# First MLP product by seven products of quarters instead of eight, in three of four chunks of inner features

## The chip, the cores and the metric

The kernel runs on one core of one Trainium2 chip. The metric is the device time of one execution, in microseconds (us): 1731.39 us before the change, the median of three runs (1730.09 to 1732.92). A core has five instruction queues that run at the same time and wait for each other by semaphores: PE (matrix products, with its weight loads, PEld), DVE (vector), ACT (scalar), POOL, and SP, which here issues DMAs. Each queue works through its list in order.

## The reference

The program is a decoder trunk of two layers over 512 tokens and 16 meta tokens, with 1024 features. Layer 0 mixes tokens by retention and gated DeltaNet heads, layer 1 by a Mamba-2 mixer. Behind each mixer comes a squared-ReLU MLP with 4096 inner features, and every sublayer ends in x <- LayerNorm(alpha * x + f(x)). The part that matters here:

```
def sq_relu_mlp(h, w1, w2):
    return jnp.square(jax.nn.relu(h @ w1)) @ w2

for i in range(DEPTH):                      # DEPTH = 2
    mix = retention_gdn_mixer(h, ...) if i % 2 == 0 else mamba2_mixer(h, ...)
    h = layer_norm(DN_ALPHA * h + mix, ln1_w[i], ln1_b[i])
    h = layer_norm(DN_ALPHA * h + sq_relu_mlp(h, mlp_w1[i], mlp_w2[i]), ln2_w[i], ln2_b[i])
```

All data are float32.

## The kernel before

Activations lie with features on the 128 partitions and tokens along the free dimension: 528 columns in layer 0 (two halves of 272 and 256) and 512 in layer 1 (behind its mixer the meta tokens are dropped). Each float32 operand is split in two tiles, a rounded high part and the low rest. A product of two operands then takes three matrix products (`mm3`, L172 to L175): high by high, high by low, low by high. Here "product" always means one of these PE instructions, and "split" the pair of a cast on ACT (L152) and a subtraction on DVE (L153).

A weight tile is 128 rows by 1024 columns, loaded by SP into one of two `wr` buffers (`fetch`), and split in two pieces of 512 columns into six `wh` and six `wl` buffers. A tile gives 128 output features and holds eight blocks of 128 inner features, so one output tile takes 8 x 3 = 24 products per stream of tokens: in layer 0 two streams (272 and 256 columns), in layer 1 one of 512 columns.

`mlp` (L376) goes over four chunks `c` of 1024 inner features. In each chunk `phase` makes eight tiles of the first product from `h` (names `hh`, `hl`), and `evac_u` turns each sum in PSUM into `u`: relu on ACT (L381), square in full precision on POOL (L383), the square's high part on ACT (L389), its low part on DVE (L390). Then a second `phase` makes eight tiles of the second product from `u`, and `evac0` (from `residual`, L363, or L367 and L368 in chunk 0) adds them on DVE to the residual sums, of which 16 tiles of the tag `m` stay in use through the whole MLP. The tags and their numbers of buffers: `s` 40 (528 columns), `m` 20, `row` 3, PSUM `mm` (names pmm) 3 and `mx` (names pmx) 5.

The order of instructions is made when the program is built: a scheduler gives each engine its list, in order of program and of readiness by its own estimate, so instructions of later tiles can stand ahead of earlier ones. On the chip that list is kept. `spawn` adds a generator whose stages are emitted one at each `tick`, between two parts of a product.

Up to the second products of layer 0's first MLP chunk the changed program has the same lists on every engine, apart from line numbers, and SP's list of DMAs is the same throughout.

Of the kernel before, what the change touches and what calls it, by code (L numbers as in the profile page):

```python
# [12 lines left out]
F32 = mybir.dt.float32  # L13
# [5 lines left out]
P = 128  # L19
# [19 lines left out]
PP_LN = 0  # L39
# [18 lines left out]
def trunk(ctx: ExitStack, tc: tile.TileContext, a, out):  # L58
# [68 lines left out]
    # ---------------------------------------------------------------- constants  # L127
# [22 lines left out]
    # ---------------------------------------------------------------- weights  # L150
# [26 lines left out]
    def product(o, blks, xs, m=P, k0=0, k1=None, every=8):  # L177
        """o[m, n] += sum over k0 <= k < k1 of blks[k]^T xs[k]"""
# [9 lines left out]
    def phase(tiles, rhs, evac, ns, head=0, tail=0, ready=None):  # L188
        """tiles: list of (srcs, key[, m]); rhs[half][k] = (hi, lo) APs, rhs[2] both halves where they fit a
        bank. In the first and the last tiles the halves are apart, so that what precedes and follows can  # L190
        work on one half at a time."""
# [28 lines left out]
    def jobs(lst, rhs, ns, **kw):  # L220
        """phase whose tiles bring their own evac"""
        phase(lst, rhs, lambda ev, hf, o: ev(hf, o), ns, **kw)

    # ---------------------------------------------------------------- h: hi/lo in two halves
# [3 lines left out]
    def parts(pair, spans):  # L228
        """(hi, lo) over the spans of both tiles"""
        return [tuple(x[:, o:o + n] for x in pair) for o, n in spans]  # L230

    # while the first loads are under way, products of zeros let the clock of the tensor engine come up
# [26 lines left out]
    def layernorm(r, ns, hf, go, apply, together=False):  # L259
        """statistics of the tokens of a half as its sums r come, then apply(off, bn, pt, mean, rstd, i)"""  # L260
# [49 lines left out]
    def norm_after(r, ns, wcol, bcol):  # L310
        """tasks for both halves, each from when its sums have been emitted"""
# [35 lines left out]
    def residual(hx, offs, ns, early=()):  # L347
        """evac into r = alpha * h + product"""
# [24 lines left out]
    def mlp(l, hx, ns, ready, r, evac0):  # L373
        w1, w2 = a["mw1"], a["mw2"]
        for c in range(4):
            u = [[None] * 8 for _ in hx]  # L376

            def evac_u(f, hf, o):
                n = ns[hf]
# [4 lines left out]
                if hf == 0:  # L384
                    pair = tl("s", L, F32R), tl("s", L, F32R)
                    for dst, x in zip(u, parts(pair, ((0, n), (n, ns[1]), (0, 512)))):
                        dst[f] = x
                hi, lo = u[hf][f]
# [3 lines left out]
            phase([([w1[l, c * 8 + f]], f) for f in range(8)], hx, evac_u, ns,  # L392
                  head=3 if c == 0 else 0, ready=ready if c == 0 else None)
            phase([([w2[l, c, m]], m) for m in range(KT)], u,
                  lambda m, hf, o: evac0(m, hf, o, last=c == 3), ns, tail=3 if c == 3 else 0)

    # ---------------------------------------------------------------- shared pieces
# [15 lines left out]
    def conv_job(src, wc, bcol, done):  # L413
        """projection through conv and silu, feature-major [128, L]"""
# [30 lines left out]
    def gate_job(src, width, task):  # L445
        """small projection, then a task on its sums"""
# [10 lines left out]
    def gate_task(fm, width):  # L457
        """token-major [128, 5, width] with unused rows zero"""
# [9 lines left out]
    def decay(dt_in, bias, alog, nh):  # L468
        """g = -exp(A_log) softplus(x + bias), sums over chunks and their exponentials"""
# [17 lines left out]
    # ================================================================ layer 0 mixer  # L487
# [475 lines left out]
    def hb(ap):  # L963
        """[128, heads] over the 64 features of a head"""
        return bc(ap, 64)
# [353 lines left out]
```

## Time and profile before

| | |
|---|---|
| median of three runs | 1731.39 us |
| the profiled execution, from its first to its last instruction | 1727.4 us |
| difference, around the span | 4.0 us |
| granted PE clock over the span | 0.995 of full speed |
| DVE splits of 512 columns (L153), whole program | 498, 759 ns on average |
| POOL squares (L383) | 128, 729 ns on average |
| relu out of PSUM (L381) | 128, 380 ns on average |
| bytes moved by DMA | 157.99 MB |

Layer 0's MLP runs from about 515 to 890 us of the span, layer 1's from about 1365 us to its end. A profile row of a timeline gives the start and the duration in us, the engine, the source line, the operation, and the tiles written <- read; "x2" means that two instructions were merged in the row, and a bracket tells how long the engine was idle ahead of it and what ended that. A row of the table by stretches gives, for each of PE, PEld, DVE, ACT and POOL in that order, the busy time and the number of instructions in the stretch, then the granted PE clock, the mean busy share of the DMA engines and GB/s. Busy times of PE overlap, since its products are pipelined; what counts for PE is the distance from start to start.

### The profile page before, as it was taken

The numbers are of one execution on the slowest core, as the hardware profiler recorded it, in microseconds if no ns is written. First come the engines' busy times: TensorE is split into PE (matmuls) and PEld (weight loads), VectorE is DVE, ScalarE is ACT, GpSimd is POOL, SyncE is SP. The second block draws the span as 40 slices with busy tenths as digits, with TensorE's granted clock in tenths as the row PEclk, the third lists the DMA queues.
The fourth block names the chain that finished last, engine by engine and source line by source line (L and its number), as shares of the span: only waits on it lengthen the run. The fifth ranks groups of instructions, "written<-read, shape, count | busy, mean of one in ns | idle before, by whom it ended". The sixth has DMA issues, their size and how long they took to land.

```text
span 1727.4 us, 29456 instructions
## 1 busy us (share of the span) xinstructions
PE 1690.1 (98%) x11644; PEld 1537.0 (89%) x11644; DVE 1015.5 (59%) x2116; ACT 680.0 (39%) x1455; POOL 324.1 (19%) x380
## 2 busy tenths in 40 slices
PE   9999999999999999999999999999999999999997
PEld 8899998899999999999999878888788888888886
DVE  6896667676436443343348767868753744444345
ACT  4432345554225333242425634554432533333331
POOL 1311211010004111010202245242400411101012
PEclk9999999999999999999999999999999999999999
DMA  7224211112222222222221443333222222222221
GB/s 252 69 86 121 77 63 62 38 63 85 98 66 82 92 92 87 98 87 89 96 72 61 131 133 88 99 110 111 80 79 98 73 86 98 98 98 89 94 98 61
DMA packets 80325, 157.99 MB, mean 91 GB/s; under 512 B 12668, under 2 KB 45820, under 8 KB 79932
## 3 DMA queue, kind: packets, MB, share of 16 engines
q1 hardware_dynamic: 80044, 155.86, 28.2%
q8 instruction: 91, 1.49, 0.4%
q14 instruction: 46, 0.38, 0.1%
q10 hardware_dynamic: 144, 0.26, 0.0%
HBM read 149.95 MB, written 6.15 MB: 90 GB/s over the span
## 4 chain that ended last, share of the span: by engine, by line
PE 84%; DVE 6%; DMA 3%; POOL 3%; ACT 2%; issue 2%; SPq 0%; POOLq 0%; DVEq 0%; ACTq 0%
PE pmm L173 24%; PE pmm L175 24%; PE pmm L174 24%; DMA row<-rd 2%; DVE s L407 2%; DVE wl L153 2%; POOL row L985 1%; PE pmx L271 1%; POOL hl L341 1%; DMA wr<-in_w 1%; PE pmx L331 1%; PE pmx L1049 1%; PE pmx L1045 1%; POOL n L147 1%; PE pmx L753 1%
## 5 line engine op out<-in xcount | busy, mean ns | idle before, releaser
L173 PE MATMUL pmm<-hh,wh 128*128 128x272 f32 (+4 forms) x2104 | 652.3, 311 | 2.3 <-ACT wh L152 0.9
L174 PE MATMUL pmm<-hl,wh 128*128 128x272 f32 (+4 forms) x2104 | 638.5, 304 | 2.7 <-POOL hl L341 2.1
L175 PE MATMUL pmm<-hh,wl 128*128 128x272 f32 (+4 forms) x2104 | 640.3, 304 | 0.1
L153 DVE TENSOR_TENSOR wl<-wr,wh 128x512 fp32r<-128x512 f32 (+1 forms) x498 | 376.2, 759 | 319.8 <-ACT wh L152 313.5
L152 ACT CAST wh<-wr 128x512 fp32r<-128x512 f32 (+1 forms) x498 | 306.6, 619 | 628.3 <-PE pmm L174 605.1
L173 PEld LDWEIGHTS pmm<-hh,wh 128*128 128x128 f32 (+2 forms) x2104 | 393.5, 187 | 25.0 <-issue 4.4
L174 PEld LDWEIGHTS pmm<-hl,wh 128*128 128x128 f32 (+2 forms) x2104 | 393.6, 187 | 24.4 <-POOL hl L341 4.6
L175 PEld LDWEIGHTS pmm<-hh,wl 128*128 128x128 f32 (+2 forms) x2104 | 393.5, 187 | 17.0 <-DVE wl L153 0.3
L173 PE MATMUL pmm<-s,wh 128*128 128x256 f32 (+2 forms) x1192 | 377.9, 317 | 0.0
L175 PE MATMUL pmm<-s,wl 128*128 128x256 f32 (+2 forms) x1192 | 377.2, 317 | 0.0
L174 PE MATMUL pmm<-s,wh 128*128 128x256 f32 (+2 forms) x1192 | 376.4, 316 | 0.0
L174 PEld LDWEIGHTS pmm<-s,wh 128*128 128x128 f32 x1192 | 224.3, 188 | 15.5 <-DVE s L1124 0.3
L173 PEld LDWEIGHTS pmm<-s,wh 128*128 128x128 f32 x1192 | 224.4, 188 | 15.1
L175 PEld LDWEIGHTS pmm<-s,wl 128*128 128x128 f32 x1192 | 224.1, 188 | 15.0
L383 POOL TENSOR_TENSOR m<-m 128x256 f32<-128x256 f32 (+1 forms) x128 | 92.1, 729 | 536.0 <-ACT m L381 532.7
L147 POOL TENSOR_TENSOR n<-n,neg 128x1 f32<-128x1 f32 (+2 forms) x58 | 37.9, 657 | 462.7 <-DVE n L146 436.5
L390 DVE TENSOR_TENSOR s<-m,s 128x256 fp32r<-128x256 f32 (+1 forms) x128 | 64.3, 521 | 95.2 <-POOL m L383 93.2
L407 DVE SCALAR_TENSOR_TENSOR s<-s,pp,s 128x528 f32<-128x528 f32 x120 | 96.5, 804 | 25.8 <-ACT s L405 24.1
L363 DVE TENSOR_TENSOR m<-m,pmm 128x256 f32<-128x256 f32 (+1 forms) x108 | 43.7, 423 | 107.4 <-PE pmm L175 107.2
L381 ACT ACTIVATE m<-pmm 128x256 f32<-128x256 f32 (+1 forms) x128 | 48.7, 380 | 60.4 <-PE pmm L175 60.4
L985 POOL TENSOR_TENSOR row<-row,m 128x1024 f32<-128x1024 f32 x16 | 32.8, 2052 | 122.3 <-DMA row<-rd 78.3
L389 ACT ACTIVATE s<-m 128x256 fp32r<-128x256 f32 (+1 forms) x128 | 54.0, 422 | 3.9
(275 smaller groups left out, 1501.1 us busy)
## 6 DMA issues: line engine op xcount, KB each, us to landing
wr<-in_mw SPq DMA_DIRECT2D x128, 512.0 KB, 3.3
wr<-in_w SPq DMA_DIRECT2D x88, 512.0 KB, 3.3
wr<-in_wo SPq DMA_DIRECT2D x29, 512.0 KB, 3.5
row<-rd SPq DMA_DIRECT2D x16, 512.0 KB, 6.0
s<-rd SPq DMA_DIRECT2D x32, 128.0 KB, 6.1
out<-row SPq DMA_DIRECT2D x7, 256.0 KB, 2.0
wr<-in_wo SPq DMA_DIRECT2D x6, 256.0 KB, 3.0
dt<-row SPq DMA_DIRECT2D x3, 365.5 KB, 5.9
```

What stands on the lines that cost most here:

```text
L147: G.tensor_tensor(dst, t, neg5[0:part, 0:n], op=POW)
L152: S.copy(dst_hi, src)
L153: V.tensor_tensor(dst_lo, src, dst_hi.bitcast(F32), op=SUB)
L173: T.matmul(o, w[0], x[0], start=first, stop=False)
L174: T.matmul(o, w[0], x[1], start=False, stop=False)
L175: T.matmul(o, w[1], x[0], start=False, stop=last)
L381: S.activation(t, o, AF.Relu)
L383: G.tensor_tensor(q, t, t, op=MUL)
L389: S.activation(hi, t, AF.Square)
L390: V.tensor_tensor(lo, q, hi.bitcast(F32), op=SUB)
L407: V.scalar_tensor_tensor(acc, cin[:, k:k + L], w[k], acc, op0=MUL, op1=ADD)
L985: G.tensor_tensor(g3(rw, 8), g3(rw, 8), bc(gc[:, c * 32 + 8 * g:c * 32 + 8 * g + 8], P), op=SUB)
```

## The change

For chunks 1 to 3 of each MLP (24 output tiles of the first product in a layer), two weight tiles and the whole token stream are taken together as a product of 2 x 2 blocks. The weight blocks are a11, a12 (tile f, inner blocks 0 to 3 and 4 to 7) and a21, a22 (tile f + 4); the blocks of h are its eight feature blocks in two groups of four, cut in two equal halves of tokens (`nh` = 264 columns in layer 0, 256 in layer 1). The blocks are combined as in Winograd's form of Strassen's method, in seven block products instead of eight:

- four sums of weight blocks for each pair of tiles: S1 = a21 + a22 and S3 = a11 - a21 on DVE, S2 = S1 - a11 and S4 = a12 - S2 on POOL, each 512 columns;
- four combinations of the blocks of h, made once in each layer (`combos`): for each of four feature blocks four steps, each a subtraction on POOL, one or two sums on DVE, and a split;
- seven block products of 4 x 3 = 12 products, 84 for a pair of tiles, where there were 96 (layer 0) or 48 of twice the width (layer 1);
- the results put together by a copy on ACT (L439) and five sums out of PSUM on DVE (L441, L445, L447, L454, L458), then `evac_u` as before on four pieces.

The order of the seven on PE in the source is a11 (first part of one output), S2, S3, S1, a12, a22, S4. The splits of S1 to S4 go to tiles of the tag `s`, eight for a pair; 16 more such tiles hold the combinations of h until the MLP ends. `p1` and `u3` are `m` tiles that hold partial sums.

```diff
+    def sevens(srcs, keys, B, nh, evac):
+        raw1, raw2 = fetch(srcs[0]), fetch(srcs[1])
+        a11, a12, a21, a22 = [x[:, i:i + 512] for x in (raw1, raw2) for i in (0, 512)]
+        s12, s34 = tl("row", 1024), tl("row", 1024)
+        s1, s2, s3, s4 = [x[:, i:i + 512] for x in (s12, s34) for i in (0, 512)]
+        V.tensor_tensor(s1, a21, a22, op=ADD)
+        V.tensor_tensor(s3, a11, a21, op=SUB)
+        G.tensor_tensor(s2, s1, a11, op=SUB)
+        G.tensor_tensor(s4, a12, s2, op=SUB)
...
+        bank = [pm(nh)] + [px(nh) for _ in range(3)]
...
+        w11 = pair(a11, False)
+        prod(bank[0], w11, 0, True, False)
+        p1 = tl("m", nh)
+        S.copy(p1, bank[0])
+        prod(bank[1], pair(s2, True), 5, True, True)
+        V.tensor_tensor(p1, p1, bank[1], op=ADD)
+        tick()
+        prod(bank[2], pair(s3, True), 6, True, False)
+        u3 = tl("m", nh)
+        V.tensor_tensor(u3, p1, bank[2], op=ADD)
+        prod(bank[3], pair(s1, True), 4, True, False)
+        V.tensor_tensor(u3, u3, bank[3], op=ADD)
+        evac(keys[1], 1, u3)
+        tick()
+        prod(bank[0], pair(a12, False), 1, False, True)
+        evac(keys[0], 0, bank[0])
+        prod(bank[2], pair(a22, False), 3, False, True)
+        c21 = tl("m", nh)
+        V.tensor_tensor(c21, p1, bank[2], op=ADD)
+        evac(keys[1], 0, c21)
+        tick()
+        prod(bank[3], pair(s4, True), 2, False, True)
+        V.tensor_tensor(p1, p1, bank[3], op=ADD)
+        evac(keys[0], 1, p1)
+        tick()
...
-            phase([([w1[l, c * 8 + f]], f) for f in range(8)], hx, evac_u, ns,
-                  head=3 if c == 0 else 0, ready=ready if c == 0 else None)
+            if c == 0:
+                phase([([w1[l, f]], f) for f in range(8)], hx, evac_u, ns, head=3, ready=ready)
...
+                spawn(combos(pairs, nh, get))
+                B += [[half(k, 0) for k in range(4)], [half(k, 0) for k in range(4, 8)],
+                      [half(k, 1) for k in range(4, 8)], tt[3], tt[0], tt[1], tt[2]]
+            else:
+                for f in range(4):
+                    sevens([w1[l, c * 8 + f], w1[l, c * 8 + f + 4]], (f, f + 4), B, nh,
+                           lambda f, hf, o: evac_u(f, hf, o, nh))
```

and the combinations of h, one of four such rounds:

```diff
+    def combos(pairs, nh, get):
...
+        for k in range(4):
+            d1, d3, e = tl("m", nh), tl("m", nh), tl("m", nh)
+            G.tensor_tensor(d1, part(k, 1, 0), part(k, 0, 0), op=SUB)
+            V.tensor_tensor(e, part(k, 1, 1), part(k, 0, 1), op=SUB)
+            V.tensor_tensor(d1, d1, e, op=ADD)
+            get(0, k, d1)
+            yield
...
+            d2, d4 = tl("m", nh), tl("m", nh)
+            G.tensor_tensor(d2, part(k + 4, 1, 0), d1, op=SUB)
+            V.tensor_tensor(d2, d2, part(k + 4, 1, 1), op=ADD)
+            get(1, k, d2)
+            yield
```

How the lists change is shown at three places. The number behind a name is that of the buffer.

First, DVE in the first product of layer 0's chunk 2, before: two tiles, of which each brings two splits of weights (L153) and two low parts of u (L390).

```order
L153 TENSOR_TENSOR wl1629_8194<-wr1627_8191,wh1628_8193 128x512
L153 TENSOR_TENSOR wl1631_8198<-wr1627_8191,wh1630_8197 128x512
L390 TENSOR_TENSOR s1597_8009<-m1600_8039,s1596_8008 128x256
L390 TENSOR_TENSOR s1610_8083<-m1608_8080,s1609_8082 128x272
L153 TENSOR_TENSOR wl1642_8268<-wr1640_8265,wh1641_8267 128x512
L153 TENSOR_TENSOR wl1644_8272<-wr1640_8265,wh1643_8271 128x512
L390 TENSOR_TENSOR s1610_8083<-m1613_8113,s1609_8082 128x256
L390 TENSOR_TENSOR s1623_8157<-m1621_8154,s1622_8156 128x272
```

The same place of the changed kernel, from the third to the fourth pair of the chunk. Ahead of these rows stand the split of S2 of the third pair, L458 of the second, the split of S3 of the third and L413 for the fourth.

```order
L153 TENSOR_TENSOR s1919_9619<-row1904_9555,s1918_9618 128x512
L486 TENSOR_TENSOR s1892_9501<-m1901_9547,s1891_9500 128x264
L441 TENSOR_TENSOR m1912_9581<-m1912_9581,pmx1907_9562 128x264
L414 TENSOR_TENSOR row1942_9719<-wr1939_9714,wr1940_9716 128x512
L445 TENSOR_TENSOR m1917_9616<-m1912_9581,pmx1908_9563 128x264
L447 TENSOR_TENSOR m1917_9616<-m1917_9616,pmx1909_9564 128x264
L486 TENSOR_TENSOR s1923_9640<-m1921_9637,s1922_9639 128x264
L486 TENSOR_TENSOR s1929_9664<-m1927_9661,s1928_9663 128x264
L153 TENSOR_TENSOR s1936_9692<-row1905_9556,s1935_9691 128x512
L454 TENSOR_TENSOR m1932_9683<-m1912_9581,pmx1908_9563 128x264
L153 TENSOR_TENSOR wl1978_9880<-wr1976_9877,wh1977_9879 128x512
L153 TENSOR_TENSOR s1951_9747<-row1941_9718,s1950_9746 128x512
```

Where before only splits and low parts alternated, the splits of S1 (first row), S4 (s1936) and the next pair's S2 (last row) now stand behind sums that read PSUM (pmx) and behind low parts of u (now L486) that need POOL's square.

Second, PE in the same chunk, from the first pair to the second, after the change. The banks are pmm1869 and pmx1870 of the second pair and pmm1906 of the third.

```order
L433 MATMUL pmm1869_9398<-hh1358_6667,wl1874_9403 128x264
L433 MATMUL pmx1870_9399<-s1539_7564,s1876_9420 128x264 [waits Activation_49]
L433 MATMUL pmx1870_9399<-s1539_7564,s1876_9420 128x264
L433 MATMUL pmm1906_9561<-hh1346_6637,wh1910_9565 128x264
L433 MATMUL pmm1906_9561<-hl1347_6638,wh1910_9565 128x264
L433 MATMUL pmm1906_9561<-hh1346_6637,wl1911_9566 128x264
L433 MATMUL pmm1906_9561<-hh1350_6647,wh1910_9565 128x264
L433 MATMUL pmm1906_9561<-hl1351_6648,wh1910_9565 128x264
L433 MATMUL pmx1870_9399<-s1539_7564,s1877_9421 128x264 [waits DVE_49]
```

Five products of the third pair's a11 stand between the first two of S2 (pmx1870, high part s1876) and its third, which waits for the low part s1877 from DVE; before, each tile's 24 products stood together, and this place has no counterpart there.

Third, DVE beside the second products of layer 0's chunk 0, one tile, before:

```order
L367 SCALAR_TENSOR_TENSOR m1567_7806<-hh1366_6687,pmm1566_7781 128x272
L368 SCALAR_TENSOR_TENSOR m1567_7806<-hl1367_6688,m1567_7806 128x272
L153 TENSOR_TENSOR wl1590_7972<-wr1588_7969,wh1589_7971 128x512
L367 SCALAR_TENSOR_TENSOR m1569_7834<-hh1366_6687,pmm1568_7809 128x256
L368 SCALAR_TENSOR_TENSOR m1569_7834<-hl1367_6688,m1569_7834 128x256
L153 TENSOR_TENSOR wl1592_7976<-wr1588_7969,wh1591_7975 128x512
```

and after:

```order
L367 SCALAR_TENSOR_TENSOR m1563_7716<-hh1358_6667,pmm1562_7691 128x272
L398 TENSOR_TENSOR m1564_7719<-m1564_7719,hl1367_6688 128x264
L368 SCALAR_TENSOR_TENSOR m1563_7716<-hl1359_6668,m1563_7716 128x272
L153 TENSOR_TENSOR s1566_7723<-m1564_7719,s1566_7723 128x264
L153 TENSOR_TENSOR wl1599_7921<-wr1597_7918,wh1598_7920 128x512
L367 SCALAR_TENSOR_TENSOR m1568_7751<-hh1358_6667,pmm1567_7726 128x256
L402 TENSOR_TENSOR m1565_7720<-m1565_7720,hl1367_6688 128x264
L368 SCALAR_TENSOR_TENSOR m1568_7751<-hl1359_6668,m1568_7751 128x256
L153 TENSOR_TENSOR wl1601_7925<-wr1597_7918,wh1600_7924 128x512
L153 TENSOR_TENSOR s1569_7756<-m1565_7720,s1569_7756 128x264
```

Each tile has got two steps of the combinations: a sum (L398, L402) behind POOL's subtraction, and the low part of a split of 264 columns.

More of the change, by code (lines that the diff above doesn't have):

```diff
@@ L371, in residual, with part, diff @@
         return r, evac
-    def mlp(l, hx, ns, ready, r, evac0):
+    def combos(pairs, nh, get):
+        q = slice(0, nh), slice(nh, 2 * nh)
+        def part(k, c, lo):
+            return pairs[k][lo][:, q[c]].bitcast(F32)
+        def diff(out, a, b, engine):
+            engine.tensor_tensor(out, a, b, op=SUB)
+        for k in range(4):
[5 more added lines that the diff above has]
+            yield
+            G.tensor_tensor(d3, part(k + 4, 1, 0), part(k, 1, 0), op=SUB)
+            V.tensor_tensor(e, part(k + 4, 1, 1), part(k, 1, 1), op=SUB)
+            V.tensor_tensor(d3, d3, e, op=ADD)
+            get(2, k, d3)
+            yield
[3 more added lines that the diff above has]
+            get(1, k, d2)
+            yield
+            G.tensor_tensor(d4, part(k + 4, 0, 0), d2, op=SUB)
+            V.tensor_tensor(d4, d4, part(k + 4, 0, 1), op=ADD)
+            get(3, k, d4)
+            yield
@@ new lines, in sevens, with pair, prod @@
+    def sevens(srcs, keys, B, nh, evac):
[7 more added lines that the diff above has]
+        G.tensor_tensor(s4, a12, s2, op=SUB)
+        def pair(x, big):
+            if big:
+                hi, lo = tl("s", 512, F32R), tl("s", 512, F32R)
+            else:
+                hi = sb.tile([P, 512], F32R, tag="wh", bufs=6, name=nm("wh"))
+                lo = sb.tile([P, 512], F32R, tag="wl", bufs=6, name=nm("wl"))
+            split(hi, lo, x)
+            return hi, lo
+        bank = [pm(nh)] + [px(nh) for _ in range(3)]
+        def prod(o, w, b, first, last):
+            for k in range(4):
+                c = slice(k * P, (k + 1) * P)
+                for i, (x, y) in enumerate(((0, 0), (0, 1), (1, 0))):
+                    T.matmul(o, w[x][:, c], B[b][k][y], start=first and k == i == 0, stop=last and k == 3 and i == 2,
+                             skip_group_check=True)
+        w11 = pair(a11, False)
[23 more added lines that the diff above has]
+        tick()
@@ L374, in mlp, with evac_u @@
+    def mlp(l, hx, ns, ready, r, evac0, pairs):
         w1, w2 = a["mw1"], a["mw2"]
+        nh = (ns[0] + ns[1]) // 2
+        B = []
         for c in range(4):
             u = [[None] * 8 for _ in hx]
-            def evac_u(f, hf, o):
-                n = ns[hf]
+            us = [None] * 8
+            def evac_u(f, hf, o, n=None):
+                off = 0
+                if n is None:
+                    n, off = ns[hf], hf * ns[0]
+                else:
+                    off = hf * n
@@ L926, in trunk @@
     r, ev = residual(h, (0, 0), ns0, early=range(5, KT))
-    hn, _, ready = norm_after(r, ns0, PP_LN, PP_LN + 8)
+    hn, hp, ready = norm_after(r, ns0, PP_LN, PP_LN + 8)
     phase([([a["wo0"][m, :, 0:1024], a["wo0"][m, :, 1024:2048]], m) for m in range(KT)], y, ev, ns0, tail=2)
@@ L931, in trunk @@
     hn, hx, ready1 = norm_after(r, ns0, PP_LN + 16, PP_LN + 24)
-    mlp(0, h, ns0, ready, r, ev)
+    mlp(0, h, ns0, ready, r, ev, hp)
     h = hn
@@ L1152, in trunk @@
     r, ev = residual(h, (16, 0), ns1, early=range(5, KT))
-    hn, _, ready = norm_after(r, ns1, PP_LN + 32, PP_LN + 40)
+    hn, hp, ready = norm_after(r, ns1, PP_LN + 32, PP_LN + 40)
     until(lambda: yw[2][11] is not None)
@@ L1216, in trunk @@
     spawn(finish(1))
-    mlp(1, h, ns1, ready, r, ev)
+    mlp(1, h, ns1, ready, r, ev, hp)
     drain()
```

18 lines of the change are left out of this document (14 added, 4 removed).

## The prediction

> **What bounds the kernel now.** I read the engine totals first, then the chain that ended last, then the stages the change touches.
>
> ```profile
> span 1727.4 us, 29456 instructions
> PE 1690.1 (98%) x11644; PEld 1537.0 (89%) x11644; DVE 1015.5 (59%) x2116; ACT 680.0 (39%) x1455; POOL 324.1 (19%) x380
> PE 84%; DVE 6%; DMA 3%; POOL 3%; ACT 2%; issue 2%; SPq 0%; POOLq 0%; DVEq 0%; ACTq 0%
> ```
>
> TensorE (PE) holds 84% of the chain. The share says nothing of the first MLP products, so next comes the table by stretches: a stretch of layer 0's first products (feature chunk 1), two tiles of layer 1's, and DVE's rows in each.
>
> ```profile
> core 0: us, PE busy (x) PEld busy (x) DVE busy (x) ACT busy (x) POOL busy (x), PEclk, DMA share, GB/s
> 623.60:670.50 46.90, 46.90 (x385) 46.90 (x385) 18.32 (x33) 21.45 (x46) 10.98 (x15) 1.00 0.28 91
> 1456.50:1467.60 11.10, 11.10 (x49) 9.02 (x49) 5.09 (x9) 5.27 (x13) 2.82 (x4) 1.00 0.28 95
> ...
> 628.69 0.44 DVE L390 TENSOR_TENSOR s<-m,s 128x272 fp32r<-128x272 f32 x1 [2.75 <-POOL m L383]
> 634.56 0.44 DVE L390 TENSOR_TENSOR s<-m,s 128x272 fp32r<-128x272 f32 x1 [2.07 <-POOL m L383]
> ...
> 1462.02 0.69 DVE L153 TENSOR_TENSOR wl<-wr,wh 128x512 fp32r<-128x512 f32 x1 [2.08 <-ACT wh L152]
> 1467.57 0.69 DVE L153 TENSOR_TENSOR wl<-wr,wh 128x512 fp32r<-128x512 f32 x1 [2.08 <-ACT wh L152]
> ```
>
> PE never stops there, and DVE is busy 18.32 of 46.90 us. The same DVE instruction recurs every 5.87 us in layer 0 (634.56 - 628.69) and every 5.55 us in layer 1: one feature tile. So a pair of tiles costs 11.74 and 11.10 us, all of it PE. A shorter product helps only while the other engines keep up.
>
> **What is removed.** A pair has 96 products of 256 or 272 columns in layer 0 (11.74 / 96 = 0.122 us each) and 48 of 512 in layer 1 (11.10 / 48 = 0.231 us). The change issues 84 per pair, of 264 columns (0.122) and of 256. The price of 256 is read in layer 1's last tiles:
>
> ```profile
> 1699.19 0.28 PE L174 MATMUL pmm<-s,wh 128*128 128x256 f32 x1
> 1704.50 0.28 PE L174 MATMUL pmm<-s,wh 128*128 128x256 f32 x1
> ```
>
> These are 45 products apart: 5.31 / 45 = 0.118 us. PE work per pair falls to 84 x 0.122 = 10.27 us (-1.47) and 84 x 0.118 = 9.91 us (-1.19). Twelve pairs a layer: 17.6 + 14.3 = **31.9 us less PE work**.
>
> The Trainium skill ("TensorE: Matmul & The Clock Gate", Back-to-back issue gap) gives sustained streams 81 ns a product at 128 columns and 131 ns at 512, which speaks against halving the width. An estimate between those two figures is about 98 ns at 256, so layer 1's pairs would go from 6.3 to 8.2 us and the change would lose some 23 us there. The rows have 0.118 beside 0.231, and I use the rows.
>
> **What is added.** Per pair: three more weight splits (7 for 4, a cast on ACT and a subtraction on DVE each), two weight sums on DVE (L413, L414), two on POOL (L415, L416), five sums out of PSUM on DVE, one copy on ACT. With the four evacuations that stay, DVE has 9 instructions of 512 columns and 9 of 264 or 256 per pair, against 4 and 4. Their pace, when the next is ready:
>
> ```profile
> 1018.19 0.69 DVE L153 TENSOR_TENSOR wl<-wr,wh 128x512 fp32r<-128x512 f32 x1
> 1018.79 0.42 DVE L1082 SCALAR_TENSOR_TENSOR s<-m,pmm 128x256 f32<-128x256 f32 x1
> 1019.12 0.69 DVE L1006 TENSOR_TENSOR s<-pmx,m 128x512 f32<-128x512 f32 x1
> ```
>
> Starts are 0.60 and 0.33 us apart, less than the durations. 9 x 0.60 + 9 x 0.34 = 8.5 us per pair, under PE's 10. But DVE and POOL get in each other's way:
>
> ```profile
> 968.76 1.90 POOL L985 TENSOR_TENSOR row<-row,m 128x1024 f32<-128x1024 f32 x1 [1.05 <-DMA row<-rd]
> 969.35 1.86 DVE L153 TENSOR_TENSOR wl<-wr,wh 128x512 fp32r<-128x512 f32 x1 [3.56 <-ACT wh L152]
> ...
> 1085.74 2.13 DVE L153 TENSOR_TENSOR wl<-wr,wh 128x512 fp32r<-128x512 f32 x2
> 1085.90 1.42 POOL L1009 TENSOR_TENSOR s<-s,s 128x512 f32<-128x512 f32 x1 [4.75 <-DVE s L1006]
> ...
> 1020.67 1.04 POOL L1009 TENSOR_TENSOR s<-s,s 128x512 f32<-128x512 f32 x1
> ...
> 1052.45 3.46 POOL L1093 TENSOR_TENSOR s<-s,s 128x512 f32<-128x512 f32 x2
> 1052.96 0.87 DVE L1053 TENSOR_TENSOR s<-s,pmx 128x128 f32<-128x128 f32 x4
> ```
>
> A split that takes 0.69 us alone took 1.86 because POOL was at work; it ended 0.55 us after POOL. In the second piece the two alternate: two splits took 2.13 us where 0.60 + 0.69 = 1.29 would do, so POOL's sum cost DVE 0.84, 0.20 less than the 1.04 that it takes alone. An operand in PSUM escapes (four L1053, 0.87 us for the four, beside POOL). So each POOL sum of 512 takes 0.84 us from DVE's two-SBUF work and each square about 0.44 (0.64 less the same 0.20), except where DVE reads PSUM or waits anyway. POOL per pair: 2 x 0.84 + 4 x 0.44 = 3.4 us. Pair on DVE: from 8.5 (nothing collides) to 11.9 us (all does). PE needs 10.3 and 9.9, so **the place inside that range decides**.
>
> The Trainium skill ("SBUF — State Buffer", SBUF: two separate sides) calls this port pair an exclusive lock, held for the whole instruction. By that rule a POOL sum costs DVE its full 1.04 and a square 0.64 us; with half of the six times 0.20 on the path, my sum would grow by 0.6 x 18 = 11 us. The rows show some overlap (0.55 after POOL's end for a split of 0.69), so the shorter values stand.
>
> DVE works in order, and the order shown above for the third chunk has 15 instructions from the split of S2's low part in one pair to that in the next: 7 of 512, 5 sums from PSUM, 3 evacuations. 7 x 0.60 + 8 x 0.34 = 6.9 us. After L447, DVE waits for relu and square:
>
> ```profile
> 633.41 0.40 ACT L381 ACTIVATE m<-pmm 128x272 f32<-128x272 f32 x1 [1.85 <-PE pmm L175]
> 633.89 0.64 POOL L383 TENSOR_TENSOR m<-m 128x272 f32<-128x272 f32 x1 [1.86 <-ACT m L381]
> ```
>
> 0.40 + 0.64 + 0.15 of gaps = 1.2 us, and the next L486 waits about 0.75 more for its own square. POOL's two sums and p1's square take 0.84 + 0.84 + 0.44 = 2.1. Sum 11.0, with a first wait on PE of 0.2 **11.2 us a step**, which is 0.9 above PE's 10.3 in layer 0 and 1.3 above its 9.9 in layer 1. PE rows pulled forward from the next pair are counted in PE's time already.
>
> Per chunk of four pairs PE then waits: three steps, 2.7 us (3.9); in the first pair, whose preparations lie in the preceding second products where DVE has room (17.96 of 46.50 us busy in the row below), 0.6 for S4 and 1.0 for the next S2, 1.6 us (1.0 in layer 1); at the end for the last sum, relu and square (0.43 + 0.40 + 0.43) and S4, less the second products put between, 1.3 us (0.3, since 512-column products cover more).
>
> ```profile
> 670.50:717.00 46.50, 46.50 (x385) 46.50 (x384) 17.96 (x32) 10.50 (x19) 0.83 (x1) 1.00 0.28 91
> L152 ACT CAST wh<-wr 128x512 fp32r<-128x512 f32 (+1 forms) x498 | 306.6, 619 | 628.3 <-PE pmm L174 605.1
> ```
>
> That is **5.6 us in layer 0 and 5.2 in layer 1**, against 5.9 and 4.8 us saved: six chunks return 32.4 us.
>
> In chunk 0 of each layer the 16 combinations of h are made beside the second products. From the first residual to S2's low part, DVE has 20 instructions of 512 and 64 of 264: 20 x 0.60 + 64 x 0.34 = 33.8 us, and POOL takes at most 16 x 0.44 + 3 x 0.84 = 9.6. PE gives it 8 x 5.87 - 3.2 (the first half tile) + 24 products of 0.122 ahead of S2's = 46.7 us in layer 0 and 8 x 5.55 - 5.8 + 32 x 0.118 = 42.4 in layer 1. It is late by nothing and by 1.0, plus round trips over POOL and ACT: 0 to 10 us, I take 3 in all, near the low end since the budget fits. DMA bytes do not change; 0.28 of the DMA share leaves room, and each pair's two tiles are fetched about two pairs ahead. Longer ACT queues (7 casts of 0.62, 9 short of about 0.4: 7.9 us a pair) stay under PE.
>
> **Sum.** 1727.4 - 31.9 + 32.4 + 3 = 1730.9 us of span; the median of the runs (1731.39) is 4.0 above the profiled span, so **1735 us**.
>
> **Rivals.**
> Faster: POOL and DVE rarely meet, as in the layer 0 stage above, where the whole DVE load met only four squares a pair. Then POOL's 2.1 us a step lie mostly under PSUM sums and waits and a step is 10.4 us: the 18 steps return 18 x 0.8 = 14.4, chunk 0 two more, 1719 us; if the first pairs' waits go too, 1711. For it: five PSUM sums a pair escape POOL. Against: POOL's sums follow DVE's in the rows and stand beside splits. It turns at a step only 0.2 us shorter than mine.
> Clearly slower: DVE goes by durations (0.69, 0.43) because each instruction waits for a neighbour. A step is 7 x 0.69 + 8 x 0.43 + 1.2 + 0.75 + 2.1 = 12.3, +1.1 x 18 = 20 us; in chunk 0, 20 x 0.69 + 64 x 0.43 + 9.6 = 50.9 us on DVE against 46.7 and 42.4 gives 13 instead of 3. 1765 us. For it: splits follow casts and sums follow sums (each waits for the end of the one before); against: most neighbours in the rows are independent.
> Buffers: 16 of 20 "m" tiles hold the residual, four are left for p1, u3, relu and square. If a relu waits 1 us more a pair for one: 24 us, 1759.
> The scheduler could keep PE's products at the old count; the order shows 84, so little is left to that.
>
> **How the numbers follow.** Chances: forecast 0.43 (1728 to 1745), few collisions 0.27, durations 0.22, buffers 0.06, no effect 0.02. The last two sides lean slower because every wait that I left out adds. About 0.2% (3.5 us) is what a measurement of this kernel tells from no change: the forecast splits into 0.20 within that and 0.23 slower. Faster 0.27, same 0.22, slower 0.51. The range runs from the lower end of the few-collisions case to the durations case: 1712 to 1766.
>
> **What would show it.** Right: PE busy falls by about 32 us while its idle time before L433 rises by about 35, put down to DVE s L153 (S4 and S2); S2-to-S2 on DVE near 11.2 us; L153 on average above 0.75 us in those stretches. Wrong: steps near 10.3 with PE dense (faster), or PE waiting over 5 us ahead of the first S2 of chunk 1 (chunk 0 mis-sized), or waits put down to ACT (m tiles).

## Result, and the profile after

The changed kernel takes 1776.41 us (median of four runs, 1775.49 to 1778.92), the kernel before 1730.74 in the same comparison: 1.0267 times as long, with a 95% interval from 1.0252 to 1.0281. That is **slower by 2.7%, 45.7 us**, where 1735 us with a range up to 1766 had been predicted. Its profiled execution has a span of 1775.1 us, 47.7 more than before.

From the page of the changed kernel, its span, the engine totals and the chain that ended last by engine:

```profile
span 1775.1 us, 30545 instructions
PE 1691.0 (95%) x11932; PEld 1546.2 (87%) x11932; DVE 1197.3 (67%) x2436; ACT 729.6 (41%) x1583; POOL 436.9 (25%) x460
PE 64%; DVE 13%; DMA 8%; ACT 6%; issue 5%; POOL 4%; SPq 0%; DVEq 0%; POOLq 0%; ACTq 0%
```

PE's share of the chain fell from 84% to 64%, and DMA's rose from 3% to 8%, although no byte more is loaded for the weights. DVE is busy 67% of the span and not full. PE's busy time is as large as before with less work. One part of this is the clock, which is lower behind some waits (last section). Another is how busy time is counted: beside a wait a product counts with its whole 0.28 to 0.39 us, in a stream only with the 0.122 us to the next.

The table by stretches over the six chunks with seven products (layer 0's chunks 1 to 3, then layer 1's), from the first to the last product of L433; columns as in the prediction, PE busy, PEld, DVE, ACT, POOL, granted clock, DMA share, GB/s:

```profile
628.10:685.90 57.80, 49.44 (x355) 47.12 (x355) 45.33 (x80) 28.71 (x66) 22.81 (x22) 0.91 0.24 84
731.50:784.30 52.80, 46.22 (x359) 44.10 (x359) 38.66 (x66) 26.35 (x60) 20.30 (x21) 1.00 0.25 86
829.80:885.00 55.20, 49.15 (x361) 47.10 (x360) 40.74 (x68) 26.55 (x60) 21.19 (x23) 0.94 0.24 82
1469.10:1526.70 57.60, 48.52 (x347) 45.33 (x346) 45.18 (x80) 29.64 (x68) 21.78 (x22) 0.94 0.25 91
1569.20:1622.70 53.50, 45.45 (x350) 42.52 (x349) 39.24 (x69) 26.23 (x60) 21.05 (x21) 1.00 0.25 84
1664.70:1717.00 52.30, 45.42 (x350) 42.46 (x349) 38.52 (x68) 26.23 (x60) 20.67 (x21) 1.00 0.25 85
```

They last 329.2 us in all. The products alone would take 1008 x 0.122 + 1008 x 0.118 = 242 us, and the second products that stand among them about 15, so some **72 us** are lost here, where the prediction had 32.4. With 31.9 us less PE work that leaves a loss of 40 us out of 47.7. Of the rest, 4 us arose in the program's first 100 us, which the change doesn't touch (in the first 50 us the granted clock was 0.93, in the profile of before 1.00), and some 4 are spread over the other stages.

Who made PE wait ahead of L433 (PE's waits over the whole span: us in total, times, the longest), and what ended the waits of the engines that read the loaded weight tiles (the rows of tile `wr`, last row: that of the kernel before):

```profile
PE pmx L433 <- ACT s L152: 22.3, 20, 4.3
PE pmx L433 <- DVE s L153: 8.2, 14, 1.0
PE pmx L433 <- DVE m L445: 7.2, 7, 2.6
PE pmm L433 <- ACT wh L152: 2.5, 3, 1.0
...
  DMA wr<-in_mw: 52.1, 29
...
  DMA wr<-in_mw: 2.7, 2
```

Most of PE's waits end with a *cast* on ACT, not with a low part on DVE, and the engines that read the weight tiles wait 52.1 us for loads where they waited 2.7. Neither was in the prediction's sum, though casts on ACT were named there as a sign of being wrong. One place shows how the two hang together; here is the timeline of the second chunk while PE works on its second pair (start, duration, engine; the first row is earlier by one pair):

```profile
732.00 1.64 POOL L416 TENSOR_TENSOR row<-wr,row 128x512 f32<-128x512 f32 x1
...
749.33 1.36 POOL L416 TENSOR_TENSOR row<-wr,row 128x512 f32<-128x512 f32 x1 [1.30 <-DVE s L153]
749.79 1.45 DVE L414 TENSOR_TENSOR row<-wr,wr 128x512 f32<-128x512 f32 x1
751.31 0.80 SPq L157 DMA_DIRECT2D wr<-in_mw  x2
754.90 0.62 ACT L152 CAST wh<-wr 128x512 fp32r<-128x512 f32 x1 [0.99 <-DMA wr<-in_mw]
755.75 0.60 ACT L152 CAST wh<-wr 128x512 fp32r<-128x512 f32 x1
756.26 0.61 ACT L152 CAST s<-row 128x512 fp32r<-128x512 f32 x1
756.92 0.39 PE L433 MATMUL pmx<-hh,s 128*128 128x264 f32 x1 [0.96 <-ACT s L152]
```

The weights run ahead: the sums at 749 are the third pair's, the loads at 751.31 the fourth's. S3's sum on DVE (L414) lies beside POOL's S4 (L416) and takes 1.45 us instead of 0.68. Only when it ends, at 751.24, are both `wr` buffers free, and SP issues the fourth pair's tiles 0.07 us later. They land at 754.90, 3.59 us after the issue, and ACT stood waiting for them, because the cast of the first of them is next in its list. The cast of the *second* pair's S4, a sum that POOL made at 732.00, stands behind two of these casts, and PE waits 0.96 us for it. ACT's list of the changed program at this place (wr1939 is a tile of the fourth pair, row1868 the second pair's S3 and S4):

```
677 L152 CAST wh1947_9728<-wr1939_9714 128x512 [waits DMAHW2_49]
678 L485 ACTIVATE s1891_9500<-m1889_9496 128x264 [waits Activation_49]
679 L152 CAST wh1961_9806<-wr1939_9714 128x512
680 L152 CAST s1898_9528<-row1868_9393 128x512
```

This is one of several ways to such waits. Of the 20 waits for the cast of an `s` tile (22.3 us), five (4.8 us) come, as here, within 4 us of a wait of ACT for a load. Two (7.1 us) stand ahead of the first S2 of chunk 1 in each layer. In the other thirteen (10.4 us) ACT had last waited for the sum of L447 on DVE: a relu (L477) that reads it stands ahead of S4's cast in ACT's list. The first pair of the same chunk:

```profile
739.78 0.42 ACT L477 ACTIVATE m<-m 128x264 f32<-128x264 f32 x1 [1.63 <-DVE m L447]
741.82 0.60 ACT L152 CAST s<-row 128x512 fp32r<-128x512 f32 x1
742.48 0.39 PE L433 MATMUL pmx<-hh,s 128*128 128x264 f32 x1 [0.99 <-ACT s L152]
```

PE's waits for L445, on the other hand, are mostly late loads: four of the seven (6.4 of 7.2 us), all in the first pair of chunks 2 and 3 of a layer. ACT waits for a tile, DVE's split of it waits for ACT's cast, and L445 stands behind that split:

```profile
837.69 0.62 ACT L152 CAST wh<-wr 128x512 fp32r<-128x512 f32 x1 [5.76 <-DMA wr<-in_mw]
838.34 0.69 DVE L153 TENSOR_TENSOR wl<-wr,wh 128x512 fp32r<-128x512 f32 x1 [3.53 <-ACT wh L152]
838.95 0.42 DVE L445 TENSOR_TENSOR m<-m,pmx 128x264 f32<-128x264 f32 x1
839.43 0.51 PE L433 MATMUL pmx<-s,wh 128*128 128x264 f32 x2 [2.07 <-DVE m L445]
```

### The profile page after: what moved, and what is told of

It is laid out like the page before. It is cut to its first block, busy times and chain, and to the rows that moved or that the text cites. A ratio compares the mean times of both kernels' runs of the same rounds, so it can differ in the third digit from the quotient of the medians.

```text
span 1775.1 us, 30545 instructions
## 1 busy us (share of the span) xinstructions
PE 1691.0 (95%) x11932; PEld 1546.2 (87%) x11932; DVE 1197.3 (67%) x2436; ACT 729.6 (41%) x1583; POOL 436.9 (25%) x460
## 4 chain that ended last, share of the span: by engine, by line
PE 64%; DVE 13%; DMA 8%; ACT 6%; issue 5%; POOL 4%; SPq 0%; DVEq 0%; POOLq 0%; ACTq 0%
PE pmm L173 17%; PE pmm L174 17%; PE pmm L175 17%; DMA wr<-in_mw 5%; DVE wl L153 3%; PE pmx L433 3%; DMA row<-rd 3%; DVE s L153 2%; ACT wh L152 2%; DVE s L522 1%; POOL row L1100 1%; DVE s L486 1%; PE pmx L271 1%; ACT s L152 1%; POOL hl L341 1%
## 5 line engine op out<-in xcount | busy, mean ns | idle before, releaser
L153 DVE TENSOR_TENSOR wl<-wr,wh 128x512 fp32r<-128x512 f32 (+1 forms) x474 | 378.5, 803 | 218.0 <-ACT wh L152 213.5
L173 PE MATMUL pmm<-hh,wh 128*128 128x256 f32 (+5 forms) x1528 | 468.6, 307 | 2.6 <-ACT wh L152 1.6
L174 PE MATMUL pmm<-hl,wh 128*128 128x256 f32 (+5 forms) x1528 | 455.8, 299 | 2.8 <-POOL hl L341 2.1
L175 PE MATMUL pmm<-hh,wl 128*128 128x256 f32 (+5 forms) x1528 | 456.2, 299 | 0.0
L173 PEld LDWEIGHTS pmm<-hh,wh 128*128 128x128 f32 (+2 forms) x1528 | 286.0, 187 | 17.7 <-issue 4.4
L174 PEld LDWEIGHTS pmm<-hl,wh 128*128 128x128 f32 (+2 forms) x1528 | 286.2, 187 | 16.0 <-POOL hl L341 4.6
L175 PEld LDWEIGHTS pmm<-hh,wl 128*128 128x128 f32 (+2 forms) x1528 | 286.0, 187 | 8.5 <-DVE wl L153 0.2
L479 POOL TENSOR_TENSOR m<-m 128x256 f32<-128x256 f32 (+2 forms) x128 | 99.6, 780 | 230.9 <-ACT m L477 226.4
L433 PE MATMUL pmx<-s,s 128*128 128x264 f32 (+1 forms) x864 | 117.8, 292 | 14.1 <-ACT s L152 7.1
L433 PEld LDWEIGHTS pmx<-s,s 128*128 128x128 f32 x864 | 112.0, 196 | 17.2 <-DVE s L153 9.4
L486 DVE TENSOR_TENSOR s<-m,s 128x256 fp32r<-128x256 f32 (+2 forms) x128 | 61.0, 480 | 65.3 <-POOL m L479 48.7
L477 ACT ACTIVATE m<-m 128x264 f32<-128x264 f32 (+1 forms) x72 | 30.3, 420 | 125.8 <-DVE m L447 97.1
```

The lines of the kernel that those rows point to most:

```text
L153: V.tensor_tensor(dst_lo, src, dst_hi.bitcast(F32), op=SUB)
L173: T.matmul(o, w[0], x[0], start=first, stop=False)
L174: T.matmul(o, w[0], x[1], start=False, stop=False)
L175: T.matmul(o, w[1], x[0], start=False, stop=last)
L433: T.matmul(o, w[x][:, c], B[b][k][y], start=first and k == i == 0, stop=last and k == 3 and i == 2, skip_group_check=True)
L477: S.activation(t, o, AF.Relu)
```

## The experiments

Fifteen of the sixteen kernels are edits of the changed one; times are medians, set beside 1776.4 us for the change and 1731 for the kernel before, which was run again with each group (1730.7 to 1732.7). With each edit the scheduler makes the lists anew: with four buffers, for example, about one in eight of ACT's instructions stands at another place. So a time belongs to the edit together with its new lists.

**1. Four buffers for the loaded tiles.**

```diff
-        raw = sb.tile([P, 1024], F32, tag="wr", bufs=2, name=nm("wr"))
+        raw = sb.tile([P, 1024], F32, tag="wr", bufs=4, name=nm("wr"))
```

> The changed kernel with four buffers for the loaded weight tiles (tag wr) in the place of two. Theory A (buffers): a pair of tiles fills both wr buffers and frees them only with its last sums of weights (L414, L416) and the splits of a12 and a22, so the next pair's tiles are issued late, land 3.5 us later, and ACT's casts, S4's cast behind them, make PE wait. With four buffers the chain of waits no longer holds wr<-in_mw in the first products of chunks 1 to 3, PE's waits ahead of L433 fall from some 45 us to under 25, and the time from 1776 to 1735 to 1755 us. Theory B (pace, as predicted): DVE's list with POOL's collisions is what a step lasts; the time stays at 1771 to 1781. Theory C (order in ACT's list: S4's cast stands behind relus that wait for PE): the time stays at 1771 to 1781 too, and the waits put down to ACT s L152 stay near 22 us.

1752.49 us: 24 us of the 46 go with the number of buffers, inside what theory A gave. The waits of ACT and DVE for `wr<-in_mw` fall from 52.1 to 7.4 us, PE's for the cast of an `s` tile from 22.3 to 7.1. But PE's waits for DVE's low parts rise from 8.2 to 18.8 us, so a second cause lies under the first.

**2. Splits ahead of the products.**

```diff
         w11 = pair(a11, False)
+        ws2, ws3, ws1 = pair(s2, True), pair(s3, True), pair(s1, True)
+        w12, w22, ws4 = pair(a12, False), pair(a22, False), pair(s4, True)
```

> The changed kernel with all seven splits of a pair written right behind its sums of weights, ahead of its products; the same instructions. Theory C: S4's cast no longer stands behind relu and squares of the same pair on ACT, so the waits put down to ACT s L152 (22 us) fall under 8 and the time to 1745 to 1757. Theory A: the wr buffers come free a few us earlier as well, so the loads in chunks 1 to 3 are issued earlier; a gain of 5 to 25 us, with the DMA share of the chain of waits smaller. Theory B: DVE's list is as long as before; 1771 to 1781.

1774.96 us, no gain that counts: only theory B's range held, and theory A's 5 to 25 us did not come either. The waits for the cast of an `s` tile fall to 8.9 us, but those for DVE rise to 16.7 + 10.2. Order alone (theory C) isn't the cause.

**3. No sums on POOL.**

```diff
-        G.tensor_tensor(s2, s1, a11, op=SUB)
-        G.tensor_tensor(s4, a12, s2, op=SUB)
+        V.tensor_tensor(s2, s1, a11, op=SUB)
+        V.tensor_tensor(s4, a12, s2, op=SUB)
```

> The changed kernel with the two sums S2 and S4 (L415, L416) on DVE instead of POOL. Theory B: a POOL sum of 512 costs DVE 0.84 us of collision and would cost 0.60 on DVE itself, so a step gets 2 x 0.24 = 0.5 us shorter: 24 pairs, 12 us less, 1761 to 1769. Theory A: the chain L413, L415, L416 ahead of the casts takes 0.6 + 0.6 where it took 1.4 + 1.5 after L413, so the wr buffers come free up to 1.5 us earlier in each pair: 10 to 30 us less, with the loads issued earlier. Theory C: 1771 to 1781.

1733.74 us: 43 us gone, more than any theory gave, by *adding* 48 instructions to DVE's list. The sum that took 1.45 us takes 0.69 here (timeline, the same place of the program):

```profile
739.74 0.69 DVE L414 TENSOR_TENSOR row<-wr,wr 128x512 f32<-128x512 f32 x1
740.35 0.42 DVE L445 TENSOR_TENSOR m<-m,pmx 128x264 f32<-128x264 f32 x1
740.68 0.68 DVE L416 TENSOR_TENSOR row<-wr,row 128x512 f32<-128x512 f32 x1
```

**4. The combinations of h alone,** with eight products in chunks 1 to 3 (the four lines that call `sevens` replaced by the `phase` of before).

> The changed kernel with the combinations of h still made beside the second products of chunk 0, but the first products of chunks 1 to 3 by eight products as before the change; the combinations are used by nothing. By the prediction chunk 0 loses 3 us in all (0 to 10): 1731 to 1741, the likeliest 1734. If the combinations were the main loss (DVE too full beside the second products): above 1750.

1728.6 us, 0.9993 of the kernel before (0.9983 to 1.0003) and 2 us under the range expected: the combinations cost nothing beside the second products.

**5. The collision without anyone who waits for POOL.** The third kernel, and POOL does two sums of the same size that nobody reads:

```diff
+        for _ in range(2):
+            G.tensor_tensor(spare, s1, s1, op=SUB)
```

> The third experiment's kernel (S2 and S4 summed on DVE, 1734 us) with two more sums of 512 columns on POOL for each pair, at the place in the program where S2 and S4 were summed, into a spare tile that nothing reads. Two ways in which POOL's sums can have cost 43 us: collision (they stretch DVE's two-SBUF work) or latency (a sum takes 1.4 to 1.7 us on POOL for 0.6 on DVE, and S2's and S4's casts and the wr buffers wait for it). Collision: most of the 43 us come back, 1760 to 1780. Latency: 1731 to 1742, since nobody waits for the spare sums. In between: each has its share.

1769.69 us: 36 of the 43 us are back. Nothing waits for these sums, so it is POOL's being at work that costs, 36 / 48 = 0.75 us a sum, not the length of its sums. POOL's row and the DVE rows beside it:

```profile
745.35 2.28 POOL L420 TENSOR_TENSOR spare<-row 128x512 f32<-128x512 f32 x2 [0.62 <-DVE row L415]
746.64 1.53 DVE L153 TENSOR_TENSOR s<-row,s 128x512 fp32r<-128x512 f32 x1
748.10 1.11 DVE L417 TENSOR_TENSOR row<-row,wr 128x512 f32<-128x512 f32 x1
```

The first is S2's split, which PE waits for: 1.53 us where 0.68 is usual. (The last row, 1.11 us, lies beside the square that follows on POOL.) The squares of POOL also stand behind the two sums in its list; that this share is small is seen in the tenth experiment.

**6 and 7. Both edits, and the buffers by themselves** (third kernel with four `wr` buffers; kernel before with four).

> The first and the third experiment together: S2 and S4 on DVE, four wr buffers. If the buffers' wait (24 us in the first experiment) is one of its own, it is gone here too: 1710 to 1722. If the slow sums on POOL were what held the buffers, the third experiment has removed most of it already: 1726 to 1736.

> The kernel before with four wr buffers: what the buffers do by themselves. Where the gain of the first experiment lies in the pairs, this is 1727 to 1734, no change; if deeper loads help the rest of the program too, under 1722.

1735.48 and 1731.46 us (0.9996 of the kernel before, 0.9986 to 1.0005). So the buffers are worth 24 us with POOL's sums in place and nothing once those sums are on DVE. POOL's sums cost 17 us where there are four buffers (1752.5 - 1735.5) and 43 where there are two: some **26 of their 43 us go with the number of buffers**. The rows above show the way for one sum, which is stretched and frees its tiles late; that it is the same for all of the 26 is not shown. New lists alone hardly make it: in experiments 6, 7, 13 and 16, too, the lists changed with the number of buffers, and the time moved by less than 3 us.

**8. DVE not waiting for squares.** The third kernel with the low part of each square (L486) put off until behind the next piece's high part, 23 `m` and three `wr` buffers.

> S2 and S4 on DVE, three wr buffers and 23 m buffers, and the low part of each square of u (L486) written behind the next piece's relu, square and high part, so that DVE does not stand waiting for POOL's square of the piece just made. In the trace of the third experiment DVE stood idle some 2.5 us a pair ahead of L486. If these waits set the step: 10 to 25 us less than the third experiment, 1708 to 1724. If PE's own work or the loads set it: 1724 to 1736.

1738.28 us, no gain, and outside both ranges. It doesn't show that these waits cost nothing, since they moved: over the six stretches DVE's idle time ahead of the low parts fell from 33 to 15 us only, and that ahead of the splits, which wait for casts, rose from 4 to 23. Buffers were added in the same edit, too.

**9 and 10. Squares off POOL** in chunks 1 to 3, on the third kernel and on the change as it is; the line in those chunks:

```diff
-                G.tensor_tensor(q, t, t, op=MUL)
+                S.activation(q, t, AF.Square)
```

> The third experiment's kernel (S2 and S4 summed on DVE, 1734 us) with the four squares of a pair (L479 in chunks 1 to 3) on ACT instead of POOL, so that POOL does nothing in the pairs. If the squares' collisions with DVE (0.44 us each by the prediction, 1.8 a pair) and their round trip over POOL are what is left above PE's own work: 1700 to 1720, faster than before. If ACT, with 1.7 us more a pair (9.6 in all), becomes the late one, or the rest is PE's short stalls on casts and low parts: 1730 to 1745.

> The changed kernel with the four squares of a pair on ACT, and the sums S2 and S4 left on POOL. If POOL's sums hurt because squares stand behind them in POOL's list (and L486 behind the squares on DVE): most of the 43 us go, 1734 to 1745. If they hurt because DVE's two-SBUF work stands still beside them: 1758 to 1772, only the squares' own share goes.

1729.87 us (0.9995 of the kernel before, 0.9984 to 1.0006), and 1765.31. Without squares POOL's two sums still cost 35 us (1765.3 - 1729.9), with no square behind them, so squares that stand waiting are not the cause. This pair of runs leaves open that the sums cost by their own length, since casts wait for them here; the fifth experiment, where nothing waits for them, answers that. Together the two leave the collision with DVE.

**11 and 12. No sums of weights at all,** with two and with four `wr` buffers:

```diff
-        V.tensor_tensor(s1, a21, a22, op=ADD)
-        V.tensor_tensor(s3, a11, a21, op=SUB)
-        G.tensor_tensor(s2, s1, a11, op=SUB)
-        G.tensor_tensor(s4, a12, s2, op=SUB)
+        s1, s2, s3, s4 = a21, a11, a22, a12
```

> The changed kernel without the four sums of weight blocks: the splits of S1 to S4 read a21, a11, a22 and a12 as they are loaded (so the first products of chunks 1 to 3 are other numbers); seven splits and 84 products a pair as before. It shows what the pairs take without any sum of weights. If the sums are the whole of what is lost: 1700 to 1712. If splits, sums out of PSUM and round trips alone already keep PE waiting some 5 us a chunk, as the prediction's waits with no POOL sum in them would: 1718 to 1732.

> The kernel without the sums of weight blocks (1763 us, and so 29 us slower than with all four sums on DVE), with four wr buffers. There every split reads the loaded tiles themselves and S4's, the last, holds them to the end of the pair, so the next pair's tiles are loaded when PE needs them (ACT waits 52 us for wr<-in_mw over the program). If the late loads are the whole of that loss: 1700 to 1722, and ACT's waits for wr<-in_mw under 10 us. If the pace of splits and round trips holds the pairs: 1740 or more.

1762.6 us, outside both expectations, and 1721.15. With *less* work the eleventh is 29 us slower than the third: S4's split, the last of a pair, now reads a loaded tile and holds its buffer until then. PE waits 12.1 us for casts of newly loaded tiles. Four buffers give 41 us back. ACT still waits 35.9 us for loads in the twelfth, not under 10 as expected, yet PE's waits for casts are gone: a wait of ACT for a load need not become one of PE.

**13 and 14. What is left without POOL:** the ninth kernel with four `wr` buffers, and the ninth with the splits of the second experiment.

> No work on POOL in the pairs (1730 us) and four wr buffers. If late loads still cost there (ACT and DVE wait 32 us for wr<-in_mw, the kernel before 2.7): 1715 to 1726, faster than before the change. If these waits cost nothing, as between the third and the sixth experiment: 1726 to 1734.

> No work on POOL in the pairs, and all seven splits of a pair written ahead of its products. PE's waits for the cast of S4 (5.7 us) and of the next tile go: 1716 to 1726. If splits that stand earlier push sums out of PSUM back, which PE's next products wait for: 1728 to 1740.

1732.57 us, nothing; and **1707.59 us, 0.9867 of the kernel before (0.9852 to 0.9882)**: faster than the kernel before by 1.3%, than the change by 3.9%, and below the range expected. Two of its stretches with seven products, layer 0's chunk 2 and layer 1's:

```profile
717.10:758.60 41.50, 41.28 (x339) 41.07 (x338) 33.28 (x68) 28.59 (x72) 0.00 (x0) 1.00 0.30 102
1520.50:1561.70 41.20, 40.47 (x338) 39.94 (x337) 32.84 (x69) 28.63 (x72) 0.00 (x0) 1.00 0.30 98
```

PE is dense: 336 x 0.122 = 41.0 and 336 x 0.118 = 39.6 us of work in 41.5 and 41.2. POOL stands at 0.00, DVE at 33 of 41 us.

**15 and 16. Which of the two edits, and the buffers once more:** splits ahead and S2, S4 on DVE but squares on POOL; and the fourteenth kernel with three `wr` buffers.

> The sums S2 and S4 on DVE, all splits of a pair written ahead of its products, and the squares left on POOL (the kernel of 1708 us has them on ACT). If the order of the splits is what the pairs were short of once POOL's sums were gone: 1708 to 1716. If the squares on POOL (their collisions with DVE, their round trip) matter as much: 1720 to 1732.

> The kernel of 1708 us with three wr buffers. PE's waits in its pairs are already short, so late loads should cost nothing any more: 1704 to 1711. If they still hold the first pair of each chunk: 1698 to 1704.

1733.85 us, 2 us above its upper range, and 1706.92. On the third kernel, the order of the splits alone is worth nothing and squares on ACT alone 4 us; the two together are worth 26:

| POOL's work in the pairs | splits as in the change | splits ahead of the products |
|---|---|---|
| sums and squares | 1776.4 | 1775.0 |
| sums | 1765.3 | not tried |
| squares | 1733.7 | 1733.9 |
| none | 1729.9 | 1707.6 |

Why the squares alone keep the order from paying is not settled: in the fifteenth kernel PE waits 9.1 us for low parts on DVE and 6.9 at the ends of chunks for a high part on ACT (L487 there), in the fourteenth 3.1 us for low parts, and this does not make up 26 us. In the profiled executions half of the difference lies in the six stretches (266.3 against 252.5 us in all) and half behind them.

## Why the prediction was wrong, step by step

Two steps of it failed: loads were priced at nothing, and the pairs by the length of DVE's list, with too little for the first pair of each chunk. The other parts of the sum held or were near.

**PE's saving of 31.9 us** was right. The products of 264 and 256 columns start 0.122 and 0.118 us apart where PE doesn't wait and has its full clock, and the stretches of the fourteenth kernel are 336 of them with little else. The figures of the Trainium skill that spoke against the half width ("TensorE: Matmul & The Clock Gate", Back-to-back issue gap) are not borne out here: 0.118 beside 0.231 at 512 columns is half.

**"Each POOL sum of 512 takes 0.84 us from DVE's two-SBUF work"** was right in mechanism and near in size: 0.75 us of the whole time for each sum that nobody reads. By the Trainium skill's exclusive lock ("SBUF — State Buffer", SBUF: two separate sides) it would be the full 1.04. Single rows lengthen by 0.77 (L414, 1.45 for 0.68) and 0.85 us (S2's split, 1.53 for 0.68), below that, but some by a little more than that, as this low part, 1.53 for 0.43:

```profile
762.10 1.75 POOL L415 TENSOR_TENSOR row<-row,wr 128x512 f32<-128x512 f32 x1
762.61 1.53 DVE L486 TENSOR_TENSOR s<-m,s 128x264 fp32r<-128x264 f32 x1
```

An estimate over the whole trace of the change: the DVE rows that lie beside POOL's 48 sums are longer than rows of their kind usually are by 37 us together, 0.77 us a sum. That this and the 0.75 us of whole time agree is in part chance, because DVE has idle time and the buffers have a share in what is lost.

**"11.2 us a step"** failed, with the 1.0 to 1.6 us for the first pair. From S2's split in one pair to that in the next, DVE's rows in the changed kernel, second chunk (S2, S3 and S1 merged in the first row):

```profile
746.12 3.07 DVE L153 TENSOR_TENSOR s<-row,s 128x512 fp32r<-128x512 f32 x3
759.43 0.68 DVE L153 TENSOR_TENSOR s<-row,s 128x512 fp32r<-128x512 f32 x1
770.85 0.68 DVE L153 TENSOR_TENSOR s<-row,s 128x512 fp32r<-128x512 f32 x1
```

That is 13.3 and 11.4 us. The second is the step whose rows the prediction counted, and there it was near. The sum behind 11.2 took that one stretch of DVE's list for every step, DVE for what PE waits for, and every other wait for hidden. DVE was busy 38.66 of 52.80 us in that chunk. PE's idle time ahead of L433 rose by some 41 us, near the 35 that the prediction named as a sign, but only 8.2 of it is put down to DVE's low parts. Counted on PE, from the last product of S4 in one pair to that in the next, a pair lasts (mean over the six chunks, in us, without the second products that stand in it; the first pair from the start of its stretch):

| | first pair | each later pair |
|---|---|---|
| predicted | 11.4 | 11.2 |
| the change | 16.7 | 11.8 |
| four buffers (experiment 1) | 14.0 | 11.5 |
| no sums on POOL (experiment 3) | 13.0 | 10.8 |
| the fourteenth kernel | 10.6 | 10.4 |

So the sum was short by 0.6 us in each later pair, and by some 5 in the first pair of each chunk, for which it had 1.0 to 1.6 us of waits. What stands in its place there are the late loads (four buffers take 2.7 us off the first pair and 0.3 off a later one), the first S2 of chunk 1, and POOL's sums. The loads close a ring: the last sums of a pair free the `wr` buffers, the load follows, then the casts and splits of that tile, then in the lists of ACT and DVE what PE needs, S4's cast or L445.

**"Each pair's two tiles are fetched about two pairs ahead"** was true as a distance, and the conclusion, that loads cost nothing, is the term that failed: four buffers give back 24 of the 41 us by which the change missed the forecast. The casts and sums of those tiles stand as far ahead in the lists of ACT and DVE, so a late load can stop work that PE needs at once. With two buffers, both taken by one pair, the next tiles can't be issued before the last sum and split have read the ones before. ACT's 7.9 us a pair "stay under PE" in the same way only as a sum. Buffers and POOL's sums taken two by two (experiments 1, 3 and 6) show that two buffers cost 26 us more beside POOL's sums than without them. What the ring is made of could be read beforehand: two `wr` buffers, two tiles a pair, 3.3 us to landing, and the order of ACT's list.

**"5.6 us in layer 0 and 5.2 in layer 1" a chunk** measured some 12. In the third experiment, without POOL's sums, the same stretches last 286.6 us, some 30 above PE's own work, or 5 a chunk: what I had priced as the whole loss, collisions included, is what remains without them. In the fourteenth kernel it is some 10 in all, so most of it goes with the order of the splits and the squares on POOL together.

**"3 in all" for chunk 0** was right for what lies there (nothing, experiment 4), but the first pair behind it was not. Chunk 1 is some 3 to 5 us longer than chunks 2 and 3 in both layers. The chain of work in time ahead of layer 0's first S2, PE's longest wait (4.3 us in the rows above):

```profile
629.82 0.61 DVE row L413
630.55 1.33 POOL row L415
631.88 1.16 POOL m L401
633.07 0.45 DVE m L402
633.85 0.62 ACT s L152
634.52 0.81 PE pmx L433 x2
```

The split of S2 stood on ACT behind a combination (L401, L402) that was still being made on POOL. The prediction named this sign ("PE waiting over 5 us ahead of the first S2 of chunk 1") and it came close to it.

**A term left out** is the clock. The stretches' granted clock is short of 1.00 by 0.09, 0.06 and 0.06 in three of the six, 57.8 x 0.09 + 55.2 x 0.06 + 57.6 x 0.06 = 12 us at most. Each time it fell behind waits of PE.

**The rivals.** Few collisions: no. DVE by full durations: its time (1765) is nearest, but not its mechanism; where nothing collides, sums keep the shorter pace (L445 starts 0.61 us after L414 in the third experiment's rows, and L416 0.33 after that). The `m` buffers: the trace of the change lists no relu (L477) that waits for a low part (L486), the reader that frees such a tile, so no. The sign "waits put down to ACT" did appear, 22.3 us, yet from the casts of S4 and of the first S2, and not from `m` tiles.

## What to carry to other kernels

When a step begins to hold a loaded tile longer, draw the ring from its last reader through the free buffer, the load and the cast back to PE, before adding up any engine's list: here POOL's sums cost 43 us with two buffers and 17 with four. Work given to an idle POOL isn't free while DVE reads two operands from SBUF; moving it to the busier DVE won 43 us. And where several short rings have about the same length, an edit that loosens only one may show nothing, as the order of the splits did until POOL was empty.

## What the runs showed of the hardware beside this

After PE's wait of 4.3 us ahead of the first S2, products of 264 columns started 0.22 us apart instead of 0.122. Rows of the stretches before and behind that wait, and behind others (from the second piece on, PE's rows show the waits, in brackets):

```profile
626.00:630.00 4.00, 4.00 (x36) 4.00 (x34) 4.00 (x11) 1.54 (x4) 0.00 (x0) 1.00 0.44 149
634.50:638.00 3.50, 3.48 (x16) 3.48 (x17) 2.78 (x5) 1.28 (x3) 1.27 (x1) 0.50 0.00 0
...
657.79 0.39 PE L433 MATMUL pmx<-hh,s 128*128 128x264 f32 x1 [0.91 <-ACT s L152]
659.30 0.39 PE L433 MATMUL pmm<-hh,wh 128*128 128x264 f32 x1 [1.00 <-ACT wh L152]
659.30:663.00 3.70, 3.70 (x18) 3.70 (x19) 2.16 (x4) 3.08 (x8) 0.63 (x1) 0.54 0.02 6
...
839.43 0.51 PE L433 MATMUL pmx<-s,wh 128*128 128x264 f32 x2 [2.07 <-DVE m L445]
840.60:844.00 3.40, 3.23 (x15) 2.92 (x15) 2.38 (x6) 2.92 (x8) 1.33 (x2) 0.51 0.00 0
...
1579.12 0.51 PE L433 MATMUL pmx<-s,wh 128*128 128x256 f32 x2 [2.58 <-DVE m L445]
1579.10:1583.00 3.90, 2.86 (x21) 2.65 (x22) 2.15 (x6) 3.08 (x7) 1.45 (x2) 1.00 0.00 0
```

The granted clock was 0.50 behind the long wait, 0.54 behind two waits of 0.91 and 1.00 us close together, 0.51 a little behind a single one of 2.07 us, and 1.00 behind a single one of 2.58 us. The Trainium skill ("TensorE: Matmul & The Clock Gate", Why this matters for your kernels) warns of idle gaps over about 3 us; the first and the last case agree, and the two between show that the clock can halve behind shorter waits too. The length of a wait alone does not decide it, and no run here tries what does.
